# Feed-forward products by Strassen's seven products on 17 of 22 feature blocks, down products in groups of four

## The chip, the cores and the metric

The kernel runs on one core of one Trainium2 chip. TensorE does matrix products, VectorE (DVE) and ScalarE (ACT) elementwise work, POOL (GpSimd) some of it, and SyncE (SP) starts most transfers. The metric is the device time of one execution in microseconds (us).

## The reference

Two blocks of a language model in float32, for 512 tokens of width 1024. The first block has two layers. Each layer mixes tokens (a short convolution in layer 0, windowed attention in layer 1, and attention to 256 memory rows in both) and then has a feed-forward part:

```
h = rmsnorm(x, norm_ffn[i])
x = x + (silu(h @ w_gate[i]) * (h @ w_up[i])) @ w_down[i]     # 1024 -> 2816 -> 1024
```

The second block (sparse attention, retention, gated merge, output norm) follows; the change leaves its computation as it is.

## The kernel before

Activations lie transposed: `x` is eight tiles (chunks) of 128 features by 512 tokens. The 2816 features of the feed-forward part are 22 blocks of 128. Every float32 product is made of three matmuls in the chip's rounded float32 type (`mm3`, L109): each operand is split into a high part, a rounded copy by ScalarE (`copy`, L64), and a low part, the difference by VectorE (`lo_of`, L73); high x high, high x low and low x high add up in one PSUM bank. `weights` (L94) loads 128 x 1024 raw words through SP's queue into one of two raw buffers (`wr`), and writes the high and low part to one of three buffers each (`wh`, `wl`). `proj` (L115) runs the 8 x 3 matmuls of 512 columns for one 128-feature output.

`ffn` (L477) works on groups of 8, 7 and 7 blocks (`FFG`, L25). For each block it computes gate and up by `proj` from the input scaled by the norm's gain (`gained`, L202); the norm's row R (`norm_row`, L431: squares and sums on POOL, a token sum on TensorE, a reciprocal root in small steps on VectorE, a broadcast) is multiplied to each result; then comes silu on ScalarE, the product on POOL, and the split. After a group it runs the eight down products (448 or 512 words a weight row) and adds each into its chunk of `x` (L504). Between group 2 and 3 of layer 0 the keys and values of layer 1's memory attention are computed (`between`, L997, `mem_kv`, L355), with layer 1's bias tables. After the stage the next part scales all eight chunks (for layer 1's mixing twice, L508 and L511; for the second block L766) and forms the norm's row again (L509, L767).

No order is written out by hand. The library that builds the kernel fixes each engine's order when the kernel is built: what stands earlier in the program goes first, and a later instruction is put ahead where the earlier ones are not ready, as far as buffers of its tag are free. A tag's count is in `bufs` (L43, L44): `pp` 2, `lg` 3, `tp` 2 and `po` 1 PSUM banks; `t` 4 and `s` 3 work tiles. At run time each engine follows its order.

Of the kernel before, what the change touches and what calls it, by code (L numbers as in the profile page):

```python
# [24 lines left out]
FFG = [(0, 8), (8, 15), (15, 22)]  # L25


class Build:

    def __init__(self, ctx, tc, T, out):
        self.tc, self.nc, self.T, self.out = tc, tc.nc, T, out
        pool = lambda n, b, **k: ctx.enter_context(tc.tile_pool(name=n, bufs=b, **k))
        self.cst = pool("cst", 1)
        self.wp = pool("wp", 1)
        self.wbufs = dict(wr=2, wh=3, wl=3)
        self.sl = pool("sl", 1)
# [4 lines left out]
        self.bufs = dict(h=16, b=16, t=4, pa=6, pb=10, q=4, v=4, x=8, R=1, s=3, sa=1, k3=2, v3=1)  # L43
        self.pbufs = dict(pp=2, lg=3, tp=2, po=1)  # L44
# [6 lines left out]
    def slot(self, tag, dtype=F32, shape=(128, 512), name="s"):  # L51
        return self.sl.tile(list(shape), dtype, name=self.nm(name), tag=tag, bufs=self.bufs[tag])
# [287 lines left out]
    def mem_rows(self, tag="pb"):  # L340
# [12 lines left out]
        return [self.split_one(x, tag, g[:, c:c + 1], name="gm") for c, x in enumerate(chunks)]  # L353
# [123 lines left out]
    def ffn(self, layer, between=None):  # L477
        nc, T = self.nc, self.T
        h = self.gained(self.x, self.gain(2 + layer))
        R = None  # L480
        tags = ["b"] * 4 + ["pb"] * 4, ["b"] * 4 + ["pa"] * 3, ["v"] * 4 + ["q"] * 2 + ["pb"]
        for g, (f0, f1) in enumerate(FFG):
            if g == 2 and between:
                between()
            act = []
            for f in range(f0, f1):
                pg = self.psum("pp")
                self.proj(pg, T["w_gate"][layer, f], h)
                if R is None:
                    _, R = self.norm_row(1e-5, f"Rf{layer}")  # L490
                z = self.slot("t", name="z")
                self.mul(z, pg, R)
                nc.scalar.activation(z, z, AF.Silu)
                pu = self.psum("lg")
                self.proj(pu, T["w_up"][layer, f], h)
                u = self.slot("t", name="u")
                self.mul(u, pu, R)
                self.mul(u, u, z, nc.gpsimd)
                tag = tags[g][f - f0]
                act.append(self.split_one(u, tag, n=512, name="act") if tag == "v" else self.split(u, tag, name="act"))  # L500
            for c in range(8):
                ps = self.psum("po" if c % 3 == 2 else "tp")
                self.proj(ps, T["w_down"][layer, c][:, f0 * 128:f1 * 128], act)
                nc.vector.tensor_tensor(self.x[c], self.x[c], ps, op=ALU.add)  # L504
# [450 lines left out]
    def finish(self, merged):  # L955
# [3 lines left out]
        gpo = [self.slot("h", name="gpo") for _ in range(2)]  # L959
        for i in range(2):  # L960
            nc.gpsimd.dma_start(gpo[i], T["norm_post"][:, i * 512:i * 512 + 512].to_broadcast([128, 512]))
        xf = [[self.slot("h", name="xf") for _ in range(2)] for _ in range(4)]
        for tb in range(4):
            for half in range(2):
                nc.gpsimd.dma_start(xf[tb][half], self.xt[:, tb, half * 512:half * 512 + 512])
# [4 lines left out]
        for cg in range(4):  # L970
            def done(tb, ps):
                sq = self.slot("t", name="sq")[:, :256]
                nc.scalar.activation(sq, ps, AF.Square, accum_out=ss[tb][:, cg:cg + 1])
                self.mul(ys[tb][cg // 2][:, cg % 2 * 256:cg % 2 * 256 + 256], ps, gpo[cg // 2][:, cg % 2 * 256:cg % 2 * 256 + 256])

            self.proj_tok(T["w_out"][cg], merged, 256, 4, done)
        for tb in range(4):
# [6 lines left out]
            for half in range(2):  # L984
                y = ys[tb][half]
                if half and tb < 3:
                    self.copy(y, y, ri)
                    nc.gpsimd.tensor_tensor(y, y, xf[tb][half], op=ALU.add)
                else:
                    self.stt(y, y, ri, xf[tb][half], ALU.mult, ALU.add)  # L990
# [70 lines left out]
def _pack(i):  # L1061
# [64 lines left out]
```

## Time and profile before

| | before |
|---|---|
| time, median of 3 runs | 1670.27 us (1667.63 to 1670.51) |
| the profiled execution's own time | 1670.48 us |
| its span, first to last instruction | 1668.7 us |
| TensorE busy | 98% of the span, 8184 matmuls |
| VectorE, ScalarE, POOL busy | 63%, 38%, 15% |
| mean granted TensorE clock | 0.995 |

The busy time of TensorE counts an instruction from its start to its modelled end, and matmuls overlap; the distance of two starts is what one costs. `PEld` is TensorE's loading of stationary operands, beside the matmuls. L12 is a line of the kernel, often that of a helper, so that a tile's name (`wl`, `gl`, `acc`) tells more than the line.

### The profile page before, as it was taken

How to read it: one execution, taken by the hardware profiler on the slowest of the kernel's cores; microseconds unless marked ns; L12 is line 12 of the kernel's file. 1: busy time of each engine (PE TensorE's matmuls, PEld its weight loads, DVE VectorE, ACT ScalarE, POOL GpSimd, SP SyncE). 2: the span in 40 equal slices, each digit the busy share in tenths (PEclk: the TensorE clock that was granted, in tenths of full speed). 3: DMA queues.
4: the chain of work that ended last, by engine and by line, in shares of the span. 5: the costliest groups of instructions: out<-in, count | busy, mean ns of one | idle time of the engine just before them, and what ended most of it. 6: DMA issues, size and time to landing. Idle time of an engine off the chain costs nothing.

```text
span 1668.7 us, 21221 instructions
## 1 busy us (share of the span) xinstructions
PE 1634.9 (98%) x8184; PEld 1374.2 (82%) x8184; DVE 1059.2 (63%) x1828; ACT 639.0 (38%) x1134; POOL 247.1 (15%) x220
## 2 busy tenths in 40 slices
PE   8999999999999999999999999998999999999997
PEld 6888888888888788888888888878788888888887
DVE  7776745444454979875434435588788977764443
ACT  5532333222333467633222223324465533333333
POOL 1111411002011600051100101351001000010010
PEclk9999999999999999999999999999999999999999
DMA  5323222322352422122332332332401122243342
GB/s 188 118 85 102 91 98 91 101 101 85 118 160 91 159 83 84 62 102 88 101 101 95 100 109 91 101 138 93 166 28 58 45 82 83 70 151 114 126 159 88
DMA packets 51557, 171.39 MB, mean 103 GB/s; under 512 B 6680, under 2 KB 6880, under 8 KB 51328
## 3 DMA queue, kind: packets, MB, share of 16 engines
q1 hardware_dynamic: 45504, 151.11, 27.3%
q0 software_dynamic: 5376, 18.82, 3.4%
q8 instruction: 64, 1.05, 0.2%
q14 instruction: 37, 0.30, 0.1%
q10 hardware_dynamic: 576, 0.11, 0.0%
HBM read 160.56 MB, written 11.81 MB: 103 GB/s over the span
## 4 chain that ended last, share of the span: by engine, by line
PE 82%; DVE 10%; issue 2%; ACT 2%; DMA 1%; POOL 1%; DVEq 0%; SPq 0%; ACTq 0%; POOLq 0%
PE pp L112 11%; PE pp L113 11%; PE pp L111 11%; PE lg L111 8%; PE lg L112 8%; PE lg L113 7%; PE tp L112 3%; PE tp L253 2%; PE tp L113 2%; PE tp L111 2%; DVE wl L75 2%; PE po L111 2%; PE po L112 2%; PE po L113 2%; PE pp L133 2%
## 5 line engine op out<-in xcount | busy, mean ns | idle before, releaser
L65 ACT ACTIVATE wh<-wr 128x1024 fp32r<-128x1024 f32 (+2 forms) x280 | 288.5, 1030 | 695.1 <-PE pp L112 228.0
L75 DVE TENSOR_TENSOR wl<-wr,wh 128x1024 fp32r<-128x1024 f32 (+2 forms) x280 | 388.7, 1389 | 55.5 <-ACT wh L65 52.3
L111 PE MATMUL pp<-gh,wh 128*128 128x512 f32 x880 | 348.0, 396 | 7.4 <-ACT wh L65 5.9
L113 PE MATMUL pp<-gh,wl 128*128 128x512 f32 x880 | 347.2, 395 | 0.6 <-DVE wl L75 0.6
L112 PE MATMUL pp<-gl,wh 128*128 128x512 f32 x880 | 346.7, 394 | 0.5 <-DVE gl L71 0.5
L111 PEld LDWEIGHTS pp<-gh,wh 128*128 128x128 f32 x880 | 166.7, 190 | 41.4 <-ACT wh L65 6.4
L113 PEld LDWEIGHTS pp<-gh,wl 128*128 128x128 f32 x880 | 166.4, 189 | 33.9 <-DVE wl L75 1.6
L112 PEld LDWEIGHTS pp<-gl,wh 128*128 128x128 f32 x880 | 166.6, 189 | 33.2 <-DVE gl L71 1.3
L111 PE MATMUL lg<-gh,wh 128*128 128x512 f32 x408 | 159.8, 392 | 0.0
L112 PE MATMUL lg<-gl,wh 128*128 128x512 f32 x408 | 159.1, 390 | 0.0
L113 PE MATMUL lg<-gh,wl 128*128 128x512 f32 x408 | 158.8, 389 | 0.0
L68 POOL TENSOR_TENSOR u<-u,z 128x512 f32<-128x512 f32 x44 | 64.8, 1472 | 549.7 <-DVE u L68 432.6
L68 DVE TENSOR_TENSOR u<-lg,Rf 128x512 f32<-128x512 f32 x44 | 30.4, 691 | 137.4 <-PE lg L113 137.3
L112 PEld LDWEIGHTS lg<-gl,wh 128*128 128x128 f32 x408 | 76.7, 188 | 16.5 <-issue 0.7
L111 PEld LDWEIGHTS lg<-gh,wh 128*128 128x128 f32 x408 | 76.6, 188 | 16.3 <-issue 0.5
L113 PEld LDWEIGHTS lg<-gh,wl 128*128 128x128 f32 x408 | 76.6, 188 | 16.1 <-issue 0.2
L112 PE MATMUL tp<-actl,wh 128*128 128x512 f32 x216 | 84.5, 391 | 0.9 <-DVE actl L75 0.9
L111 PE MATMUL tp<-acth,wh 128*128 128x512 f32 x216 | 84.1, 389 | 0.0
L113 PE MATMUL tp<-acth,wl 128*128 128x512 f32 x216 | 84.1, 389 | 0.0
L68 DVE TENSOR_TENSOR z<-pp,Rf 128x512 f32<-128x512 f32 x44 | 30.4, 691 | 69.5 <-PE pp L113 65.7
L504 DVE TENSOR_TENSOR x<-x,tp 128x512 f32<-128x512 f32 x36 | 24.6, 683 | 65.5 <-PE tp L113 65.5
L71 DVE SCALAR_TENSOR_TENSOR gl<-x,gains,gh 128x512 fp32r<-128x512 f32 x40 | 52.9, 1338 | 0.5 <-ACT gh L65 0.5
(422 smaller groups left out, 3088.9 us busy)
## 6 DMA issues: line engine op xcount, KB each, us to landing
wr<-in_w_gate_dram SPq DMA_DIRECT2D x44, 512.0 KB, 3.2
wr<-in_w_up_dram SPq DMA_DIRECT2D x44, 512.0 KB, 3.2
wr<-in_w_in_dram SPq DMA_DIRECT2D x44, 512.0 KB, 3.2
wr<-in_w_down_dram SPq DMA_DIRECT2D x32, 448.0 KB, 3.3
wr<-in_a_w_in_dram SPq DMA_DIRECT2D x18, 512.0 KB, 3.2
wr<-in_w_down_dram SPq DMA_DIRECT2D x16, 512.0 KB, 3.5
wr<-in_a_w_out_dram SPq DMA_DIRECT2D x8, 512.0 KB, 3.2
wr<-in_b_w_q_dram SPq DMA_DIRECT2D x8, 512.0 KB, 3.2
```

The lines of the kernel that those rows point to most:

```text
L65: self.nc.scalar.activation(out, in_, AF.Copy, scale=scale)
L68: (eng or self.nc.vector).tensor_tensor(out, a, b, op=ALU.mult)
L71: (eng or self.nc.vector).scalar_tensor_tensor(out, a, s, b, op0=op0, op1=op1)
L75: self.nc.vector.tensor_tensor(out, x, hi.bitcast(F32), op=ALU.subtract)
L111: mm(ps, ah, bh, start=start, stop=False)
L112: mm(ps, ah, bl, start=False, stop=False)
L113: mm(ps, al, bh, start=False, stop=stop)
L133: mm(ps, a, wh, start=k == 0, stop=False)
L253: self.nc.tensor.transpose(ps[:, c:c + 128], src, self.ident)
L504: nc.vector.tensor_tensor(self.x[c], self.x[c], ps, op=ALU.add)
```

## The change

Five blocks (`PLAIN`) of each layer stay as they were, except that their sign is flipped and the down products are subtracted from `x`. For the other 17, gate and up together are one product of a 2 x 2 arrangement: the rows are gate and up, the inner halves are the even and odd chunks of the input, the columns are tokens 0 to 255 and 256 to 511. It is computed by seven products of 4 x 3 matmuls of 256 columns (`gate_up`), in which running sums in PSUM are copied out between products. The seven combinations of the scaled and normalised input are built once a layer after block 0 (`halves`); the weights' four sums are built for each block (`pair_weights`) and take the room of the scaled input, whose eight high and low tiles are joined to eight of 1024 columns.

The groups are 4, 4, 4, 4, 3 and 3 blocks. A group's eight down products (pairs of chunks share one weight load) run inside the blocks of the next group, after the fifth and the seventh product; those of the last group run at the end. The memory keys and values and the bias tables of layer 1 come after layer 0's stage, and use other buffers for their input. The weights are laid out anew to suit this. The last function of the kernel takes its tiles from the joined buffers (not shown).

```diff
-FFG = [(0, 8), (8, 15), (15, 22)]
+FFG = [(0, 4), (4, 8), (8, 12), (12, 16), (16, 19), (19, 22)]
+PLAIN = 5
...
     def slot(self, tag, dtype=F32, shape=(128, 512), name="s"):
+        if tag == "h":
+            shape = (128, 1024)
         return self.sl.tile(list(shape), dtype, name=self.nm(name), tag=tag, bufs=self.bufs[tag])
...
     def split(self, x, tag, scale=None, n=512, name="s"):
-        hi = self.slot(tag, F32R, name=name + "h")
-        lo = self.slot(tag, F32R, name=name + "l")
+        if tag == "h":
+            t = self.slot(tag, F32R, name=name)
+            hi, lo = t[:, :512], t[:, 512:]
+        else:
+            hi = self.slot(tag, F32R, name=name + "h")
+            lo = self.slot(tag, F32R, name=name + "l")
         self.copy(hi[:, :n], x, 1.0 if scale is None else scale)
         self.lo_of(lo[:, :n], x, hi[:, :n], scale)
...
-    def ffn(self, layer, between=None):
+    def halves(self, x, R, gain):
+        nc = self.nc
+        tags = iter(["pa"] * 6 + ["pb"] * 10 + ["q"] * 4 + ["v"] * 8)
+        spare = []
+        def slot(name):
+            tag = next(tags)
+            if tag != "v":
+                return self.slot(tag, F32R, name=name)
+            if not spare:
+                t = self.slot("v", F32R, (128, KWORDS), name)
+                spare.extend([t[:, :512], t[:, 512:1024]])
+            return spare.pop(0)
+        sub = lambda out, a, b: nc.vector.tensor_tensor(out, a, b, op=ALU.subtract)
+        sets = []
+        for j in range(len(x) // 2):
+            a, b, m, t = self.slot("t", name="b1"), self.slot("t", name="b2"), self.slot("s", name="m12"), self.slot("s", name="t34")
+            for c, o in ((2 * j, a), (2 * j + 1, b)):
+                self.stt(o, x[c], gain[:, c:c + 1], R, ALU.mult, ALU.mult)
+            b11, b12, b21, b22, m1, m2, t3, m4 = (o[:, u:u + 256] for o in (a, b, m, t) for u in (0, 256))
+            one = slot("B11")
+            self.copy(one[:, :256], b11)
+            self.lo_of(one[:, 256:], b11, one[:, :256])
+            sub(m1, b11, b12)
+            self.stt(m2, b22, -1.0, m1, ALU.mult, ALU.subtract)
+            sub(t3, b22, b12)
+            self.stt(m4, m2, -1.0, b21, ALU.mult, ALU.subtract)
+            parts = []
+            for o in (b, m, t):
+                h, l = slot("Bh"), slot("Bl")
+                self.copy(h, o)
+                self.lo_of(l, o, h)
+                parts.append(((h[:, :256], l[:, :256]), (h[:, 256:], l[:, 256:])))
+            (p21, p22), (p1, p2), (p3, p4) = parts
+            sets.append([(one[:, :256], one[:, 256:]), p21, p1, p2, p3, p22, p4])
+        return [[s[i] for s in sets] for i in range(7)]
+    def pair_weights(self, src):
+        nc = self.nc
+        k = lambda t: t.rearrange("p (k c) -> p k c", k=4)
+        raw = [self.wp.tile([128, 1120], F32, name=self.nm("wr"), tag="wr", bufs=self.wbufs["wr"])[:, :1024] for _ in range(2)]
+        for i, r in enumerate(raw):
+            nc.sync.dma_start(r, src[:, 1024 * i:1024 * i + 1024])
+        a22, a11, a12, a21 = (r[:, u:u + 512] for r in raw for u in (0, 512))
+        ah, al = (self.wp.tile([128, WMAX], F32R, name=self.nm(t), tag=t, bufs=self.wbufs[t])[:, :1024] for t in ("wh", "wl"))
+        self.copy(ah, raw[0])
+        self.lo_of(al, raw[0], ah)
+        res = {n: (k(ah[:, s]), k(al[:, s])) for n, s in (("a22", slice(0, 512)), ("a11", slice(512, 1024)))}
+        def put(name, x):
+            hi, lo = self.split(x, "h", name=name)
+            res[name] = k(hi), k(lo)
+        def put_sum(name, a, b):
+            t = self.slot("s", name=name)
+            nc.vector.tensor_tensor(t, a, b, op=ALU.add)
+            put(name, t)
+            return t
+        put("a12", a12)
+        s1 = put_sum("s1", a21, a22)
+        s2 = put_sum("s2", s1, a11)
+        put_sum("s3", a11, a21)
+        put_sum("s4", s2, a12)
+        return res
+    def gate_up(self, src, B, between):
+        nc, w = self.nc, self.pair_weights(src)
+        mm = nc.tensor.matmul
+        b11, b21, m1, m2, t3, b22, m4 = B
+        def product(ps, a, b, start):
+            for j in range(4):
+                (ah, al), (bh, bl) = (a[0][:, j], a[1][:, j]), b[j]
+                mm(ps, ah, bh, start=start and j == 0, stop=False, skip_group_check=not start)
+                mm(ps, ah, bl, start=False, stop=False, skip_group_check=not start)
+                mm(ps, al, bh, start=False, stop=j == 3, skip_group_check=not start)
+        U, Y, Z = (self.psum(t)[:, :256] for t in ("pp", "lg", "lg"))
+        g, u = self.slot("t", name="g"), self.slot("t", name="u")[:, :256]
+        g1, g2 = g[:, :256], g[:, 256:]
+        add = lambda out, a, b: nc.vector.tensor_tensor(out, a, b, op=ALU.add)
+        product(U, w["a11"], b11, True)
+        self.copy(g1, U)
+        product(Y, w["a12"], b21, True)
+        add(g1, Y, g1)
+        product(U, w["s2"], m2, False)
+        self.copy(g2, U)
+        product(Z, w["s1"], m1, True)
+        product(U, w["s3"], t3, False)
+        self.copy(u, U)
+        add(u, Z, u)
+        between(0)
+        product(Z, w["s4"], b22, False)
+        add(g2, Z, g2)
+        nc.scalar.activation(g, g, AF.Silu)
+        product(U, w["a22"], m4, False)
+        between(1)
+        act = self.slot("t", name="act")
+        self.mul(act[:, :256], U, g1)
+        self.mul(act[:, 256:], u, g2)
+        return self.split(act, "b", name="act")
...
+    def ffn(self, layer):
         nc, T = self.nc, self.T
-        h = self.gained(self.x, self.gain(2 + layer))
-        R = None
-        tags = ["b"] * 4 + ["pb"] * 4, ["b"] * 4 + ["pa"] * 3, ["v"] * 4 + ["q"] * 2 + ["pb"]
+        gain = self.gain(2 + layer)
+        h = self.gained(self.x, gain)
+        R = B = act = None
+        def down(i, act, g):
+            f0, f1 = FFG[g]
+            n = f1 - f0
+            w = []
+            def one(c):
+                if not w:
+                    w.extend(self.weights(T["w_down"][layer, i][:, f0 * 256:f1 * 256], 2 * n, 128))
+                ps = self.psum("po" if i % 2 else "tp")
+                self.proj(ps, None, act, [t[:, c * n:c * n + n] for t in w])
+                x = self.x[2 * i + c]
+                nc.vector.tensor_tensor(x, x, ps, op=ALU.subtract)
+            return [lambda: one(0), lambda: one(1)]
         for g, (f0, f1) in enumerate(FFG):
-            if g == 2 and between:
-                between()
+            last = act
+            todo = [] if last is None else [p for i in range(4) for p in down(i, last, g - 1)]
             act = []
+            share = -(-len(todo) // (f1 - max(f0, PLAIN - 1))) if todo else 0
             for f in range(f0, f1):
...
+                mine = []
+                if f >= PLAIN - 1:
+                    mine, todo = todo[:share], todo[share:]
+                def between(i):
+                    for p in mine[i * (len(mine) // 2):] if i else mine[:len(mine) // 2]:
+                        p()
+                if f < PLAIN:
+                    a, R = self.plain_gate_up(layer, f, h, R)
+                    between(0)
+                    between(1)
+                    if f == 0:
+                        B = self.halves(self.x, R, gain)
+                else:
+                    a = self.gate_up(T["w_gu"][layer, f - PLAIN], B, between)
+                act.append(a)
+        for i in range(4):
+            for p in down(i, act, len(FFG) - 1):
+                p()
...
     def run(self):
         self.load_consts()
         self.mrs = None
         self.layer_a()
-        def between():
-            loaded = self.bias_loads()
-            self.mem1 = self.mem_kv(1)
-            self.bias_tables(loaded)
-        self.ffn(0, between)
+        self.ffn(0)
+        loaded = self.bias_loads()
+        self.mem1 = self.mem_kv(1)
+        self.bias_tables(loaded)
         self.layer_b()
         self.ffn(1)
         self.second()
...
+    a["w_gate"] = np.stack([_feat(m[:, :PLAIN * 128]) for m in w["w_gate"]])
+    a["w_up"] = np.stack([_feat(m[:, :PLAIN * 128]) for m in w["w_up"]])
+    gate, up = (np.stack([_feat(m[:, PLAIN * 128:]) for m in w[n]]).reshape(2, 22 - PLAIN, 128, 4, 2, 128) for n in ("w_gate", "w_up"))
+    a["w_gu"] = np.stack([up[..., 1, :], gate[..., 0, :], gate[..., 1, :], up[..., 0, :]], 3).reshape(2, 22 - PLAIN, 128, 2048)
+    down = np.stack([_feat(m) for m in w["w_down"]]).reshape(2, 4, 2, 128, 22, 128).transpose(0, 1, 3, 2, 4, 5)
+    a["w_down"] = np.concatenate([down[:, :, :, :, f0:f1].reshape(2, 4, 128, -1) for f0, f1 in FFG], 3)
```

## Rows read from the trace of the kernel before

**Rows 1.** The page, part 1: busy us (share of the span) and instructions of each engine.

```profile
PE 1634.9 (98%) x8184; PEld 1374.2 (82%) x8184; DVE 1059.2 (63%) x1828; ACT 639.0 (38%) x1134; POOL 247.1 (15%) x220
```

**Rows 2.** TensorE's waits by line: us in total, times, longest; first and last.

```profile
PE pp L111 <- ACT wh L65: 5.9, 2, 5.7
...
PE lg L234 <- DVE q L210: 0.2, 1, 0.2
```

**Rows 3.** Windows: length, busy us of five engines, clock, DMA share, GB/s.

```profile
199.00:570.90 371.90, 371.26 (x1680) 307.63 (x1679) 193.99 (x219) 119.75 (x157) 56.39 (x48) 1.00 0.34 109
...
540.00:580.00 40.00, 39.25 (x177) 32.30 (x177) 37.94 (x37) 19.09 (x25) 29.09 (x27) 1.00 0.46 150
```

**Rows 4.** Timeline of TensorE: start us, duration us; 512-column matmuls, ten apart.

```profile
299.70 0.39 PE L111 MATMUL po<-acth,wh 128*128 128x512 f32 x1
...
301.97 0.39 PE L112 MATMUL po<-actl,wh 128*128 128x512 f32 x1
```

**Rows 5.** The same view, 256-column matmuls, eighteen apart.

```profile
451.80 0.28 PE L111 MATMUL lg<-gm,wh 128*128 128x256 f32 x1
...
453.96 0.28 PE L133 MATMUL tp<-wh,gm 128*128 128x256 f32 x1
```

**Rows 6.** Groups by line and shape: busy us, mean ns | idle before.

```profile
L65 ACT ACTIVATE wh<-wr 128x1024 fp32r<-128x1024 f32 x234 | 248.1, 1060 | 572.4 <-PE pp L112 217.7 <-PE lg L112 143.0 <-issue 84.4
...
L75 DVE TENSOR_TENSOR actl<-u,acth 128x512 fp32r<-128x512 f32 x36 | 24.5, 682 | 22.1 <-ACT acth L65 22.1
...
L65 ACT ACTIVATE acth<-u 128x512 fp32r<-128x512 f32 x36 | 22.8, 633 | 56.1 <-POOL u L68 56.1
...
L75 DVE TENSOR_TENSOR tp<-tp,tp 128x256 fp32r<-128x256 f32 x28 | 11.8, 420 | 3.1 <-ACT tp L65 2.7
...
L65 ACT ACTIVATE tp<-tp 128x256 fp32r<-128x256 f32 x28 | 10.6, 379 | 13.0 <-PE tp L253 12.9
```

**Rows 7.** Timeline of VectorE at the front of layer 0's feed-forward stage.

```profile
201.06 0.75 DVE L71 SCALAR_TENSOR_TENSOR gl<-x,gains,gh 128x512 fp32r<-128x512 f32 x1
...
206.03 0.16 DVE L68 TENSOR_TENSOR rt<-rt,m 128x4 f32<-128x4 f32 x1
206.11 1.23 DVE L75 TENSOR_TENSOR wl<-wr,wh 128x1024 fp32r<-128x1024 f32 x1
207.25 0.15 DVE L71 SCALAR_TENSOR_TENSOR rz<-rt,ri 128x4 f32<-128x4 f32 x1
```

**Rows 8.** Timeline of POOL and VectorE inside the stage.

```profile
234.81 1.29 POOL L68 TENSOR_TENSOR u<-u,z 128x512 f32<-128x512 f32 x1 [9.62 <-DVE u L68]
234.86 2.32 DVE L75 TENSOR_TENSOR wl<-wr,wh 128x1024 fp32r<-128x1024 f32 x1 [0.23 <-ACT wh L65]
```

**Rows 9.** The page, part 6: weight loads, KB each, us to landing.

```profile
wr<-in_w_gate_dram SPq DMA_DIRECT2D x44, 512.0 KB, 3.2
```

**Rows 10.** Timeline of VectorE, POOL and ScalarE around the end of layer 1.

```profile
1091.45 0.67 DVE L504 TENSOR_TENSOR x<-x,tp 128x512 f32<-128x512 f32 x1
...
1093.05 1.53 DVE L71 SCALAR_TENSOR_TENSOR gl<-x,gg,gh 128x512 fp32r<-128x512 f32 x1
...
1096.35 0.67 DVE L504 TENSOR_TENSOR x<-x,po 128x512 f32<-128x512 f32 x1
...
1109.47 0.67 DVE L157 TENSOR_TENSOR acc<-acc,sq 128x512 f32<-128x512 f32 x1
...
1092.20 1.82 POOL L148 TENSOR_TENSOR sq<-x 128x512 f32<-128x512 f32 x1 [1.24 <-DVE x L504]
...
1094.56 1.31 POOL L157 TENSOR_TENSOR acc<-acc,sq 128x512 f32<-128x512 f32 x1
...
1119.33 0.60 ACT L65 ACTIVATE R<-tp 128x512 f32<-128x512 f32 x1 [4.41 <-PE tp L197]
```

**Rows 11.** Timeline of TensorE after layer 1, and the window around it.

```profile
1110.20 1.95 PE L165 MATMUL tp<-ones,acc 128*128 128x2 f32 x16 [0.76 <-DVE acc L157]
...
1110.00:1120.00 10.00, 9.80 (x42) 7.89 (x43) 5.88 (x34) 1.66 (x2) 0.00 (x0) 0.83 0.39 133
```

More of the change, by code (lines that the diff above doesn't have):

```diff
@@ L338, in bias, with mem_rows @@
         return b
-    def mem_rows(self, tag="pb"):
+    def mem_rows(self):
         nc, T = self.nc, self.T
@@ L352, in mem_rows @@
         g = self.gain(5)
-        return [self.split_one(x, tag, g[:, c:c + 1], name="gm") for c, x in enumerate(chunks)]
+        res = []
+        for c, x in enumerate(chunks):
+            if c % 2 == 0:
+                t = self.slot("v", F32R, (128, KWORDS), "gm")
+            hi, lo = (t[:, a:a + 256] for a in (512 * (c % 2), 512 * (c % 2) + 256))
+            self.copy(hi, x, g[:, c:c + 1])
+            self.lo_of(lo, x, hi, g[:, c:c + 1])
+            res.append((hi, lo))
+        return res
     def mem_kv(self, layer):
@@ new lines, in pair_weights @@
+    def pair_weights(self, src):
[22 more added lines that the diff above has]
+        put_sum("s4", s2, a12)
+        return res
@@ new lines, in plain_gate_up @@
+    def plain_gate_up(self, layer, f, h, R):
+        T = self.T
+        pg = self.psum("pp")
+        self.proj(pg, T["w_gate"][layer, f], h)
+        if R is None:
+            _, R = self.norm_row(1e-5, f"Rf{layer}")
+        z = self.slot("t", name="z")
+        self.mul(z, pg, R)
+        self.nc.scalar.activation(z, z, AF.Silu)
+        pu = self.psum("lg")
+        self.proj(pu, T["w_up"][layer, f], h)
+        u = self.slot("t", name="u")
+        self.stt(u, pu, -1.0, R, ALU.mult, ALU.mult)
+        self.mul(u, u, z, self.nc.gpsimd)
+        return self.split(u, "b", name="act"), R
@@ L482, in ffn @@
         for g, (f0, f1) in enumerate(FFG):
-            if g == 2 and between:
-                between()
+            last = act
+            todo = [] if last is None else [p for i in range(4) for p in down(i, last, g - 1)]
             act = []
+            share = -(-len(todo) // (f1 - max(f0, PLAIN - 1))) if todo else 0
             for f in range(f0, f1):
[L487 to L504, printed above, removed]
+                mine = []
[4 more added lines that the diff above has]
+                        p()
@@ L958, in finish @@
         gf = self.gain(6)
-        gpo = [self.slot("h", name="gpo") for _ in range(2)]
+        gpo = self.slot("h", name="gpo").rearrange("p (i c) -> p i c", i=2)
         for i in range(2):
-            nc.gpsimd.dma_start(gpo[i], T["norm_post"][:, i * 512:i * 512 + 512].to_broadcast([128, 512]))
-        xf = [[self.slot("h", name="xf") for _ in range(2)] for _ in range(4)]
+            nc.gpsimd.dma_start(gpo[:, i], T["norm_post"][:, i * 512:i * 512 + 512].to_broadcast([128, 512]))
+        xf = [self.slot("h", name="xf").rearrange("p (i c) -> p i c", i=2) for _ in range(4)]
         for tb in range(4):
             for half in range(2):
-                nc.gpsimd.dma_start(xf[tb][half], self.xt[:, tb, half * 512:half * 512 + 512])
+                nc.gpsimd.dma_start(xf[tb][:, half], self.xt[:, tb, half * 512:half * 512 + 512])
         eps = self.const("eps", [128, 1])
@@ L987, in finish @@
                     self.copy(y, y, ri)
-                    nc.gpsimd.tensor_tensor(y, y, xf[tb][half], op=ALU.add)
+                    nc.gpsimd.tensor_tensor(y, y, xf[tb][:, half], op=ALU.add)
                 else:
-                    self.stt(y, y, ri, xf[tb][half], ALU.mult, ALU.add)
+                    self.stt(y, y, ri, xf[tb][:, half], ALU.mult, ALU.add)
                 nc.sync.dma_start(self.out[tb * 128:tb * 128 + 128, half * 512:half * 512 + 512], y)
```

7 lines of the change are left out of this document (2 added, 5 removed).

## The prediction

> **What bounds the kernel now.** I read the page's busy shares first, then who TensorE waits for, then the two feed-forward stages, then single matmuls. In the profiled execution (1670.48 us, span 1668.7, so 1.8 us lie around the span; the median of the runs shown is 1670.27, 0.2 us away, so a sum made on one holds for the other) TensorE is busy 98% of the span, VectorE 63%, ScalarE 38% [rows 1]. All of TensorE's waits that the trace names, 16 lines from 5.9 us down to 0.2 us, add up to 24 us [rows 2]. In layer 0's feed-forward stage it is busy 371.26 of 371.90 us while VectorE is busy 194 [rows 3]. So the stage is as long as its matmuls, and only a cheaper set of matmuls, or a new wait, moves the end. What such a matmul costs is the distance of two starts, since the printed duration overlaps with the next: ten of 512 columns take 301.97 - 299.70 = 2.27 us, 227 ns each [rows 4]; eighteen of 256 columns, each with its own weights, take 453.96 - 451.80 = 2.16 us, 120 ns each [rows 5]. Half the columns are thus 53% of the time: both are columns/2.4 GHz and 13.3 ns more.
>
> **Part 1, the products.** A feature block's gate and up take 2 x 8 x 3 = 48 matmuls of 512 columns: 48 x 0.2267 = 10.88 us. By seven products they are 7 x 4 x 3 = 84 of 256: 84 x 0.120 = 10.08 us. The gain is 0.80 us a block and, with 17 blocks in each of 2 layers, 34 x 0.80 = **27.2 us**, all on the path. The down products keep their 24 matmuls a block (5.44 us). The count of operations falls by an eighth (1.36 us of 10.88); two fifths of that go back into the 36 more matmuls.
> The rows say 13.3 ns a matmul beyond its columns [rows 4, 5]. The Trainium skill, "TensorE: Matmul & The Clock Gate" (section "Wait — 56ns, not 53.3ns?"), states about 2.5 ns for it, measured on other operands. By that figure the block would go from 10.35 to 9.17 us and the 34 blocks would give 40 us; the trace disagrees, and the measured 13.3 stands.
>
> **Part 2, what the blocks add off TensorE.** VectorE, per new block, by [rows 6, 7]: low part of 1024 weights 1.23; five low parts of 512 at 0.68; four sums of 512 at 0.68; three sums and two products of 256 at 0.42; the activation's low part 0.68; the down weights' low part 1.23; and, as the groups go from 3 to 6, two residual updates a block at 0.68 instead of one: 1.23 + 3.41 + 2.73 + 2.10 + 0.68 + 1.23 + 1.36 = 12.7 us. TensorE needs 10.08 + 5.44 = 15.5 us a block, so VectorE is 82% full and hides it. The gated product leaves POOL, which helps: beside a POOL product a low part of 1024 took 2.32 us, not 1.23 [rows 8]. ScalarE: 2 x 1.06 + 5 x 0.63 + 3 x 0.38 + 2 x 0.63 = 7.7 us, half full.
> Inside a block three matmul runs wait for a reader. The third and the fifth product write on into the bank that ScalarE copies out after the first and third; the other bank's product, 12 x 0.120 = 1.44 us, covers the copy (0.38 and two hand-overs of 0.23, as between a copy and its low part in [rows 8]: 0.84). Only where a 1.06 us weight copy stands ahead on ScalarE is it late, by up to 0.46. At none it costs 0; at both waits of each block 34 x 0.92 = 31 us. Such weight copies fill 2.1 of 15.5 us, so I take 14% x 0.23 x 2 = 0.07 a block, **+2.3 us**. The wait of the sixth product lies behind a down product of 12 x 0.227 = 2.7 us: nothing.
> The two raw weight buffers now carry three loads a block (two of the pair, one of down). The loop is: load 3.2 [rows 9], six VectorE steps until the last sum that reads the first buffer (6 x 0.68 = 4.1, and 0.8 of the running block's), down load 3.2, down's copy and low part 1.06 + 0.23 + 1.23 and a queue of 0.3: 14.1 us against 15.5. It fits with 1.4 to spare; I take 0, ends 0 and 1.0 us a block (34 us), the latter if more of the block's 5.4 us of other VectorE work falls into the loop.
>
> **Part 3, the combinations of the input.** They are built once in a layer when the norm's row R is there, and stand in the program before block 1's weights: per pair of chunks two scalings at 0.75 [rows 7], one low part, two differences and two scaled differences of 256 at 0.42, three low parts at 0.68: 5.64 us, times 4 = 22.6 us of VectorE. Then until the first new block TensorE has four plain blocks and two down products, 4 x 10.88 + 5.44 = 49 us. VectorE has in that time 22.6, 2.1 of block 0, 4 x (2 x 1.23 + 3 x 0.68) = 18, down 2.6, the first pair of weights 1.23 + 3.41 + 2.73 = 7.4 and five POOL products at 1.1 of delay [rows 8], less two low parts done ahead (2.5): 55.7 us. It is 6.7 us too much, but the pair's last sums are needed only 5.8 and 9.9 us into the block. The question is whether the plain blocks' low parts get between the combinations. Rows of the same engine say that they do: a low part of a later projection (206.11) stands between two steps of the norm (206.03, 207.25) that are earlier in the program [rows 7]. Ends: nothing; or none gets between, then TensorE has weights for block 1 alone, until 212 + 2 x 5.44 = 222.9, and waits until 212.9 + 22.6 + 1.5 = 237: 14 us a layer. I take 2 us a layer, near the lower end because of that row: **+4 us**. TensorE would start again at half clock (below).
>
> **Part 4, the ends of the layers.** The last down group is 3 blocks wide instead of 7. The eight final chunks then come every 9 x 0.227 = 2.04 us instead of 4.76, 16.3 us instead of 38. That helps nobody: the work per chunk is already VectorE's limit here. It is busy 37.9 of 40 us at the end of layer 0 [rows 3], and a chunk takes it 1091.45 to 1096.35, 4.9 us [rows 10]. Total work does not change, so it sticks out behind the last down product. End of layer 1: POOL works from 1092.20 to 1095.87, 3.7 us a chunk beside VectorE [rows 10]; I estimate 3.2 where VectorE is in its way less, so its sum is there at 2 + 8 x 3.2 = 28 us, and R 10 us after the sum (1109.47 to 1119.33): 38 us. TensorE has 16.3 of down, two projections (two banks) 10.9 and what of the value products has other banks, 6.2: 33.4. So 4.6 us of wait and 1.7 of clock: at this place TensorE waited 0.76 us, ran tiny matmuls, and was then granted 0.83 of its clock over ten us, 1.7 us lost between the levels 2.4 and 1.2 GHz [rows 11]. Before, the two were 2.5 us. Net +4. End of layer 0: VectorE needs eight updates at 0.67, four down low parts at 0.95 (between 0.68 for 512 and 1.23 for 1024), for the memory keys and values, now here, sixteen low parts of 256 at 0.42, four of 1024 weights at 1.23 and sixteen small steps at 0.16, then eight scaled low parts at 1.5 [rows 10] and two of weights at 1.23: 5.4 + 3.8 + 14.2 + 12 + 2.5 = 38 us; TensorE has 16.3 + 11.5 (96 matmuls of 256) + 5.4 = 33. Net +4. Together **+8 us**; ends -1 (the memory products fill the old 0.75 us wait and nothing sticks out) and +20 (10 each, nothing but the two projections covers).
>
> Sum: -27.2 + 2.3 + 0 + 4 + 8 = -12.9; 1670.5 - 12.9 = **1657.6 us**.
>
> **Rivals.** *All the additions hide* (VectorE's gaps suffice at the layers' fronts and ends): -27.2 + 2.3 = 1645.6. For it: VectorE idles half of the stage [rows 3]; against: it is full exactly where part 4 adds. *The ends eat more*: +20 instead of 8 gives 1669.6, no change. *The combinations hold VectorE*: 28 instead of 4 gives 1681.6, slower. It decides from the point where the stall passes 17 us in both layers together; program order speaks for it, the row at 206.11 against. *The raw-buffer loop sets the block*: from 15.5 + 0.4 us on it takes the whole net gain; at 16.5 us, 34 x 1.0 = 34: 1691.6, slower. Three loads in two buffers speak for it, the sum of 14.1 against. *The change does not cut the matmuls*, because the extra weight loads rule: the 256-column rows carry a fresh weight load each and still start every 120 ns, so I give it nothing.
>
> **Chances.** Forecast 0.41 (own range 1650 to 1665), all hidden 0.22, ends 0.10, combinations 0.14, loop 0.13. The predicted time is the forecast's, 1657.6. The range 1643 to 1687 takes in the first four and leaves out most of the loop case and the edge below. Measurement can tell about 0.2% (3.3 us) from no change: faster 0.62, same 0.11, slower 0.27.
>
> **What would show it.** Right: 9408 matmuls instead of 8184; the new products' starts 120 ns apart; VectorE about 80% full inside the stage; TensorE's busy share near 100% between about 60 us into the stage and its last block. Part 3: TensorE waits on VectorE's low parts (line of lo_of) within 40 us of R. Part 4: waits on scaled low parts or R's copy within 25 us of the last down product, with a granted clock under 1. The loop: ScalarE waiting on weight loads in every block, and TensorE on the pair's sums. The prediction is wrong if a block inside the stage takes more than 15.9 us, or if the fronts of the layers lose more than 10 us each.

## The result and the profile after

The changed kernel takes 1708.33 us (median of four executions) against 1670.28 for the kernel before beside it: ratio 1.0227, 95% interval 1.0207 to 1.0247. It is some 38 us slower; 12.9 us faster was predicted. One of the four executions was a slow one of 7116.75 us, so the ratio and every gain on the change below go by the other three (1706.03 to 1709.18, median 1707.48).

The page of the changed kernel, part 1 (answers to [rows 1]):

```profile
PE 1629.6 (95%) x9408; PEld 1423.0 (83%) x9408; DVE 1253.8 (73%) x2330; ACT 757.4 (44%) x1404; POOL 193.7 (11%) x186
```

TensorE has its 9408 matmuls and is busy 5 us less than before, in a span that is 38.6 us longer (1707.3). So it stood idle 44 us longer (77.7 against 33.8). And its busy time fell by 5 us where the products alone were to take 27.2 off: the mean granted clock is 0.979, before it was 0.995. In the two feed-forward stages it is busy 727.6 us; in e9 below, with the same number of matmuls and fewer waits, 711.8. The waits of the changed kernel, by line (answers to [rows 2], where the longest line was 5.9 us in all):

```profile
PE pp L120 <- DVE z L73: 14.0, 2, 7.0
PE pp L122 <- DVE wl L80: 8.0, 5, 7.0
PE pp L120 <- ACT wh L70: 7.6, 3, 5.6
PE pp L575 <- ACT g L70: 7.0, 4, 2.7
PE po L120 <- DVE x L638: 5.8, 5, 1.7
PE lg L122 <- DVE wl L80: 4.8, 2, 2.4
```

To place them, cut both executions at the ScalarE copy of each norm's row: Rf opens a feed-forward stage (twice), Rb layer 1's mixing, R the second block. The copies by tile (xcount: shortest/median/longest ns, first to last start in us), before and then after:

```profile
L65 ACT ACTIVATE Rf<-tp x2: 597/598/598, 210.8 to 754.6; 128x512 f32<-128x512 f32 x2
L65 ACT ACTIVATE Rb<-tp x1: 598/598/598, 583.8 to 583.8; 128x512 f32<-128x512 f32 x1
L65 ACT ACTIVATE R<-tp x1: 600/600/600, 1119.3 to 1119.3; 128x512 f32<-128x512 f32 x1
```

```profile
L70 ACT ACTIVATE Rf<-tp x2: 597/598/598, 209.9 to 777.0; 128x512 f32<-128x512 f32 x2
L70 ACT ACTIVATE Rb<-tp x1: 599/599/599, 599.2 to 599.2; 128x512 f32<-128x512 f32 x1
L70 ACT ACTIVATE R<-tp x1: 593/593/593, 1158.0 to 1158.0; 128x512 f32<-128x512 f32 x1
```

The differences give this ledger, with the kernels of the experiments below beside them (us, one profiled execution each):

| kernel | feed-forward 0 (Rf to Rb) | mixing 1 (Rb to Rf) | feed-forward 1 (Rf to R) | R to the end |
|---|---|---|---|---|
| before | 373.0 | 170.8 | 364.7 | 549.4 |
| after | 389.3 | 177.8 | 381.0 | 549.3 |
| e1 spread | 376.5 | 177.1 | 365.8 | 549.3 |
| e2 last six | 382.0 | 171.6 | 372.9 | 548.4 |
| e3 bias | 392.0 | 172.0 | 379.5 | 548.7 |
| e4 all three | 369.1 | 171.5 | 360.4 | 548.1 |
| e8 e1 and e2 | 371.8 | 171.7 | 360.5 | 549.8 |
| e11 after, squares moved | 387.2 | 171.0 | 370.7 | 552.1 |
| e9 e4, squares moved | 363.1 | 171.5 | 355.3 | 549.4 |
| e12 before, squares moved | 372.1 | 170.8 | 362.7 | 549.5 |

Each feed-forward stage is 16.3 us longer. With the 13.6 us that 17 cheaper blocks should have given, 29.9 us are lost in each, and 7.0 in layer 1's mixing, which the prediction did not look at.

**Inside the stage all is well.** TensorE's first product of two neighbouring new blocks (start, duration), and the window around them (columns as in [rows 3]):

```profile
293.30 0.28 PE L575 MATMUL pp<-B,wh 128*128 128x256 f32 x1
...
308.86 0.28 PE L575 MATMUL pp<-B,wh 128*128 128x256 f32 x1
```

```profile
290.00:550.00 260.00, 258.95 (x1773) 241.16 (x1773) 189.50 (x310) 119.89 (x199) 0.53 (x1) 1.00 0.31 101
```

A block takes 15.56 us; 15.52 was worked out. A plain block with its down products would take 72 x 0.2267 = 16.32, so a new one saves 0.76 here. VectorE is 73% busy and TensorE 258.95 of 260 us.

**The front.** VectorE of the changed kernel after layer 0's Rf (start, duration, operation; 16 us of combinations left out), TensorE beside it, and the window of both:

```profile
214.21 1.22 DVE L80 TENSOR_TENSOR wl<-wr,wh 128x1024 fp32r<-128x1024 f32 x1
217.26 0.69 DVE L80 TENSOR_TENSOR actl<-u,acth 128x512 fp32r<-128x512 f32 x1 [1.84 <-ACT acth L70]
217.87 0.42 DVE L80 TENSOR_TENSOR B<-b,B 128x256 fp32r<-128x256 f32 x1
...
234.17 0.68 DVE L73 TENSOR_TENSOR z<-pp,Rf 128x512 f32<-128x512 f32 x1
...
236.57 1.97 DVE L80 TENSOR_TENSOR wl<-wr,wh 128x1024 fp32r<-128x1024 f32 x1
```

```profile
235.00 0.77 PE L120 MATMUL pp<-g,wh 128*128 128x512 f32 x1 [6.97 <-DVE z L73]
...
238.59 0.79 PE L122 MATMUL lg<-g,wl 128*128 128x512 f32 x1 [2.40 <-DVE wl L80]
```

```profile
230.00:250.00 20.00, 12.60 (x40) 9.66 (x41) 13.42 (x20) 6.25 (x10) 3.63 (x2) 0.66 0.26 81
```

The number in brackets is the idle time before the instruction and what ended it. From 217.26 to 236 VectorE has not a gap. One low part of weights gets between the combinations (214.21), the next only at 236.57, and block 1's product with the norm's row (z) at 234.17. TensorE waits 6.97 and 2.40 us, and its mean granted clock over those 20 us is 0.66: matmuls on either side of the second wait take 0.63 us and more instead of 0.39, at 1.2 GHz.

**The end.** VectorE and GpSimd while the last down products of layer 0 run (answers to [rows 10], where a scaled low part took 1.53 us):

```profile
557.80 0.67 DVE L638 TENSOR_TENSOR x<-x,po 128x512 f32<-128x512 f32 x1
558.40 4.16 DVE L76 SCALAR_TENSOR_TENSOR g<-x,gains,g 128x512 fp32r<-128x512 f32 x2
562.49 0.74 DVE L76 SCALAR_TENSOR_TENSOR gl<-x,gains,gh 128x512 fp32r<-128x512 f32 x1
...
566.61 0.68 DVE L638 TENSOR_TENSOR x<-x,tp 128x512 f32<-128x512 f32 x1
...
570.29 2.93 DVE L76 SCALAR_TENSOR_TENSOR g<-x,gains,g 128x512 fp32r<-128x512 f32 x1
```

```profile
559.11 1.05 POOL L157 TENSOR_TENSOR sq<-x 128x512 f32<-128x512 f32 x1
...
560.69 1.31 POOL L166 TENSOR_TENSOR acc<-acc,sq 128x512 f32<-128x512 f32 x1
...
566.15 1.69 POOL L166 TENSOR_TENSOR acc<-acc,sq 128x512 f32<-128x512 f32 x1
...
570.37 1.30 POOL L166 TENSOR_TENSOR acc<-acc,sq 128x512 f32<-128x512 f32 x1
571.62 1.05 POOL L157 TENSOR_TENSOR sq<-x 128x512 f32<-128x512 f32 x1
```

The same low part takes 0.74 us at 562.49, behind the sum that ended at 562.00 and ahead of GpSimd's next square (564.56), and 2.93 at 570.29, beside a sum and a square of GpSimd (570.37 to 572.67). The update of x, which reads one of its operands from PSUM, keeps its 0.68 us at 566.61, inside a sum of GpSimd. Layer 1's end, TensorE and the ten us ahead of that wait:

```profile
1140.55 0.80 PE L122 MATMUL pp<-g,wl 128*128 128x512 f32 x1 [6.98 <-DVE wl L80]
```

```profile
1130.00:1140.00 10.00, 3.23 (x13) 2.36 (x13) 9.38 (x8) 3.01 (x4) 7.70 (x9) 0.94 0.13 52
```

**Layer 1's mixing.** Transfers of the changed kernel (KB each, middle of the us to landing), and what waited for them on ScalarE and TensorE:

```profile
band<-band POOLq DMA_DIRECT2D x1, 2304.0 KB, 13.3
...
wr<-in_w_kv_v_dram SPq DMA_DIRECT2D x2, 512.0 KB, 8.7
```

```profile
607.81 1.06 ACT L70 ACTIVATE wh<-wr 128x1024 fp32r<-128x1024 f32 x1 [7.99 <-DMA wr<-in_w_kv_v_dram]
...
608.92 0.39 PE L142 MATMUL pp<-wh,gh 128*128 128x256 f32 x1 [2.84 <-ACT wh L70]
```

The two loads went out at 593.5 and 594.9 us and the broadcast (`band`) at 594.20; the first load landed in 4.5 us, the second, behind the broadcast, in 12.8. In the kernel before the broadcast went out at 463.07, and both loads landed in 4.1.

### The profile page after: what moved, and what is told of

The parts are those of the page before. It is cut to its first block, busy times and chain, and to the rows that moved or that the text cites. A ratio compares the mean times of both kernels' runs of the same rounds, so it can differ in the third digit from the quotient of the medians.

```text
span 1707.3 us, 24407 instructions
## 1 busy us (share of the span) xinstructions
PE 1629.6 (95%) x9408; PEld 1423.0 (83%) x9408; DVE 1253.8 (73%) x2330; ACT 757.4 (44%) x1404; POOL 193.7 (11%) x186
## 3 DMA queue, kind: packets, MB, share of 16 engines
q1 hardware_dynamic: 45504, 151.11, 27.2%
## 4 chain that ended last, share of the span: by engine, by line
PE 72%; DVE 15%; DMA 5%; issue 3%; ACT 3%; POOL 1%; DVEq 0%; SPq 0%; ACTq 0%; POOLq 0%
PE pp L122 7%; PE pp L121 7%; PE pp L120 6%; PE lg L120 4%; DVE wl L80 4%; PE lg L122 4%; PE lg L121 4%; PE po L120 3%; PE pp L575 3%; PE pp L577 3%; PE pp L576 3%; PE po L121 3%; PE po L122 3%; DMA wr<-in_w_gu_dram 3%; PE tp L262 2%
## 5 line engine op out<-in xcount | busy, mean ns | idle before, releaser
L70 ACT ACTIVATE wh<-wr 128x1024 fp32r<-128x1024 f32 (+3 forms) x246 | 251.9, 1024 | 376.6 <-PE pp L121 150.5
L80 DVE TENSOR_TENSOR wl<-wr,wh 128x1024 fp32r<-128x1024 f32 (+3 forms) x246 | 315.9, 1285 | 63.3 <-ACT wh L70 62.6
L120 PE MATMUL pp<-g,wh 128*128 128x512 f32 x592 | 235.8, 399 | 21.9 <-DVE z L73 14.0
L122 PE MATMUL pp<-g,wl 128*128 128x512 f32 x592 | 235.0, 397 | 7.9 <-DVE wl L80 7.8
L121 PE MATMUL pp<-g,wh 128*128 128x512 f32 x592 | 234.4, 396 | 0.3 <-DVE g L76 0.3
L120 PEld LDWEIGHTS pp<-g,wh 128*128 128x128 f32 x592 | 112.5, 190 | 44.4 <-ACT Bh L70 14.7
L122 PEld LDWEIGHTS pp<-g,wl 128*128 128x128 f32 x592 | 112.1, 189 | 31.0 <-DVE wl L80 10.3
L121 PEld LDWEIGHTS pp<-g,wh 128*128 128x128 f32 x592 | 112.5, 190 | 21.4 <-DVE g L76 1.0
L70 ACT ACTIVATE s<-s 128x512 fp32r<-128x512 f32 x136 | 85.0, 632 | 49.2 <-DVE s L555 46.4
L80 DVE TENSOR_TENSOR s<-s,s 128x512 fp32r<-128x512 f32 x136 | 90.1, 682 | 1.0 <-ACT s L70 0.8
L575 PE MATMUL pp<-Bh,s 128*128 128x256 f32 x272 | 78.8, 290 | 7.3 <-ACT g L70 7.0
L577 PE MATMUL pp<-Bh,s 128*128 128x256 f32 x272 | 78.0, 287 | 0.0
L577 PE MATMUL lg<-Bh,s 128*128 128x256 f32 x272 | 77.0, 283 | 0.0
L575 PE MATMUL lg<-Bh,s 128*128 128x256 f32 x272 | 76.9, 283 | 0.0
L596 ACT ACTIVATE g<-g 128x512 f32<-128x512 f32 x34 | 21.4, 631 | 100.9 <-DVE g L582 100.9
```

Of the source, the lines that this page charges most:

```text
L70: self.nc.scalar.activation(out, in_, AF.Copy, scale=scale)
L80: self.nc.vector.tensor_tensor(out, x, hi.bitcast(F32), op=ALU.subtract)
L120: mm(ps, ah, bh, start=start, stop=False)
L121: mm(ps, ah, bl, start=False, stop=False)
L122: mm(ps, al, bh, start=False, stop=stop)
L575: mm(ps, ah, bh, start=start and j == 0, stop=False, skip_group_check=not start)
```

## The experiments

The theory at first: the combinations at the front, the narrow last group and the broadcast of the bias that moved behind layer 0's stage cost the some 64 us that lie between -27 and +38. Rivals: it is VectorE's total work, or the products themselves. Ratios are to the kernel before, run beside each.

**e1: combinations spread.** `halves` yields one pair of chunks at a time, and each of blocks 0 to 3 takes one:

```diff
-            sets.append([(one[:, :256], one[:, 256:]), p21, p1, p2, p3, p22, p4])
+            yield [(one[:, :256], one[:, 256:]), p21, p1, p2, p3, p22, p4]
...
-                        B = self.halves(self.x, R, gain)
+                        sets, parts = [], self.halves(self.x, R, gain)
+                    if f < 4:
+                        sets.append(next(parts))
...
```

> Only the place of the input's combinations changes: the set of one pair of chunks is built after each of the plain blocks 0 to 3, instead of all four after block 0. The work is the same. Theory A (their place in VectorE's order holds back block 1's gate row product and its weights): of the stall at each layer's front, 7.0 us for the gate product, 2.4 us for a low part and some 3 us of half clock, nearly all goes, 12 us a layer: 1708 - 24 = 1684 us. Rival B (VectorE simply has too much to do before the first new block, 55.7 us of work in 49): the wait moves to the first new block but stays, 5 to 7 us a layer less at best: 1695 to 1708 us.

1680.94 us, 1.0062 (1.0047 to 1.0077): 26.5 us less than the change, with the same operations on every engine. VectorE after the first pair:

```profile
218.53 0.69 DVE L80 TENSOR_TENSOR Bl<-b,Bh 128x512 fp32r<-128x512 f32 x1
219.13 0.68 DVE L73 TENSOR_TENSOR z<-pp,Rf 128x512 f32<-128x512 f32 x1
219.73 1.22 DVE L80 TENSOR_TENSOR wl<-wr,wh 128x1024 fp32r<-128x1024 f32 x1
```

Block 1's z comes at 219.13 instead of 234.17. The place in the program cost some 27 us, not the work. One thing e1 does not separate: z takes one of the four `t` tiles, and the combinations take two of them a pair, so as one block they stand ahead of z for tiles too. The weights' low part that follows z takes none of these tiles; its high part was begun at 217.13 in the changed kernel, and it came at 236.57 all the same.

**e2: last group of six.** The groups 3 and 3 become 6, and each of its down products takes its own weight load:

```diff
-FFG = [(0, 4), (4, 8), (8, 12), (12, 16), (16, 19), (19, 22)]
+FFG = [(0, 4), (4, 8), (8, 12), (12, 16), (16, 22)]
...
+                if n > 4:
+                    self.proj(ps, T["w_down"][layer, i][:, f0 * 256 + c * n * 128:f0 * 256 + (c + 1) * n * 128], act)
...
```

> Only the last two groups of three blocks are joined to one of six, so that the eight final chunks come every 18 x 0.227 = 4.08 us instead of 2.04; each final chunk loads its own weights. Theory A (the last chunks come faster than VectorE and POOL can take them, and TensorE waits behind): 10 us less at the end of layer 0 and of layer 1 each, R is there about 10 us earlier against the last block: 1708 - 16 = 1692 us. Rival B (the ends are long because the work after R has to be done anyway): no change beyond 3 us, 1705 to 1711.

1686.11 us, 1.0091 (1.0075 to 1.0108), 21.4 less. By the ledger 7.3 and 8.1 of it lie in the two stages and 6.2 in layer 1's mixing, where nothing was edited. There both loads go out ahead of the broadcast, at 582.0 and 583.4 against 588.69, and land in 4.3 us instead of 8.7:

```profile
band<-band POOLq DMA_DIRECT2D x1, 2304.0 KB, 11.7
...
wr<-in_w_kv_v_dram SPq DMA_DIRECT2D x2, 512.0 KB, 4.3
```

**e3: bias ahead of the first stage.**

```diff
+        self.bias_tables(self.bias_loads())
         self.ffn(0)
-        loaded = self.bias_loads()
         self.mem1 = self.mem_kv(1)
-        self.bias_tables(loaded)
```

> Only layer 1's bias tables (their loads, the product and the 2304 KB broadcast) are put before layer 0's feed-forward stage instead of behind it. Theory A (the broadcast takes the transfers' time from the value weights of the windowed attention, which landed 8.7 us after issue, and TensorE stands 7 us between Rb and Rf1): the stretch from Rb to Rf1 falls from 177.8 to 171 us: 1708 - 7 = 1701 us. Rival B (the stretch is longer because of VectorE's backlog after the stage): it stays at 177, 1707 us.

1705.32 us, 1.0205 (1.019 to 1.0221), 2.2 less: mixing 1 shrinks by 5.8, as theory A had it, and feed-forward 0 grows by 2.7 (from 389.3 to 392.0) and the time ahead of it by 1.2, which it had not.

**e4: all three, and e8: the bias put back.** e4 holds the three edits; e8 is e4 without e3's.

> The three edits together: sets spread over blocks 0 to 3, last group of six, bias tables ahead of the stage. Theory A (three separate waits): the gains add up, 24 + 16 + 7 = 47: 1661 us, below the 1670 of the kernel before, because the seven products themselves save 27 us. Rival B (VectorE's amount of work): at least 1690 us.

> As e4, with the loads and tables of the bias back behind the first FFN, where the change put them. Theory A (the broadcast of 2304 KB beside the loads of layer B's weights holds TensorE's first products there, some 3 to 6 us): e4 plus 3 to 6 us, 1666 to 1669 us. Rival B (ahead of the FFN it costs as much, in VectorE and POOL work beside the combinations, as it saves behind): within 1.5 us of e4.

e4: 1662.89 us, 0.9952 (0.9937 to 0.9967). e8: 1663.47, 0.9962 (0.9947 to 0.9976), the time that its rival B named, though not for B's reason: there is next to nothing to save behind the stage. Mixing 1 is 171.7 us in e8 with the broadcast where the change put it; it goes out at 578.90 there, behind the loads (572.1 and 573.5), which land in 4.3 us. The 7 us were a meeting of two transfers, not a price of the move. e1 and e2 together give 44.0, alone 26.5 + 21.4 = 47.9: they share some 4.

**e6: fewer of the new blocks.** e4 with `PLAIN = 13` (the block from which down products start kept at 4).

> As e4, with 13 plain feature blocks per layer instead of 5, so 9 by seven products instead of 17: 16 blocks go back, and all else (groups, halves, ends, bias) stays as in e4. Theory A (the products save what the starts say, 48 x 0.2267 = 10.88 less 84 x 0.120 = 10.08 us, 0.80 us a block, while a wait-free block stays on TensorE's pace): e4 plus 12.8 us, 1673 to 1678 us. Rival B (the seven products lose again on VectorE what they save, so that a block costs the same either way): within 3 us of e4. Rival C (they cost more than they save): below 1660 us.

1680.64 us, 1.0062 (1.0047 to 1.0077): 17.7 us more than e4 for 16 blocks, beyond the 12.8 that the starts say. TensorE's waits for x, 7.4 us in four times in e4, became

```profile
PE po L120 <- DVE x L639: 14.6, 12, 3.1
```

which is 7.2 more, while its waits for g fell from 4.7 to 0.7. Both rivals fall, and theory A's range (1673 to 1678) is passed as well. In the profiled executions e6 is 16.3 us longer than e4: 14.2 in the two stages and 2.2 behind them, where nothing was edited. Without the 3.2 us of waits that it has more, 11.0 of the 14.2 are left, near the 12.8 predicted. So e6 fits the saving, but does not measure it apart from the waits.

**e5 and e7: the waits that e4 still has.** e5 puts the last group's down products in three banks in turn; e7 adds a sixth plain block.

```diff
-                ps = self.psum("po" if i % 2 else "tp")
+                ps = self.psum("po" if (2 * i + c) % 3 == 2 and n > 4 or i % 2 and n <= 4 else "tp")
```

> As e4 (products and plain blocks as changed, halves spread over four blocks, last group of six, bias tables before the first FFN), and the down pieces of the last group go to the banks tp, tp, po in turn instead of tp, tp, po, po. Theory A (the 7.4 us that TensorE waits for x at the single po bank in e4, four times, is time on the path, with the half clock behind it): e4 less 6 to 8 us, 1655 to 1657 us, and the waits of po for x under 2 us in sum. Rival B (the subtraction of x on VectorE sets the pace of the last pieces whatever the bank, so the wait moves to tp): within 2 us of e4, 1661 to 1665 us.

> As e5, with 6 plain blocks per layer instead of 5: one more plain block between the last combination and the first block that uses them. Theory A (in e4 the first new block of a layer waits 2.3 us for ACT's copies of g, at half clock behind it, because VectorE and ACT still carry combinations): the two waits of 2.4 us go, with some 2 us of half clock each, and two blocks give back 0.8 us each, net 4 to 7 us below e5. Rival B (the wait belongs to the first of such blocks wherever it stands: its weights' seven low parts come late since nothing of it can run ahead): the wait stays at 2 us, and the kernel is 1 to 2 us slower than e5.

e5: 1662.02 us, 0.9953 (0.9938 to 0.9968), within e4's spread (1659.95 to 1664.07): theory A falls and rival B's time holds. The waits for x are gone from its list, but others stand in it:

```profile
PE tp L174 <- DVE acc L166: 4.4, 1, 4.4
PE tp L144 <- DVE wl L80: 3.7, 2, 2.9
```

e7: 1665.33, 0.9967 (0.9955 to 0.9979), 3.3 more than e5, though its runs spread (1661.43 to 1667.65). The wait for g went (5.5 to 0.8 us), but a down product of the added plain block waited instead:

```profile
279.09 0.50 PE L120 MATMUL po<-acth,wh 128*128 128x512 f32 x1 [2.10 <-DVE x L639]
```

Neither theory had it so. VectorE of e4 shows what sets the pace of the last pieces:

```profile
548.25 0.68 DVE L639 TENSOR_TENSOR x<-x,tp 128x512 f32<-128x512 f32 x1
548.84 1.21 DVE L80 TENSOR_TENSOR wl<-wr,wh 128x1024 fp32r<-128x1024 f32 x1
549.98 1.52 DVE L76 SCALAR_TENSOR_TENSOR gl<-x,gains,gh 128x512 fp32r<-128x512 f32 x1
551.43 1.90 DVE L76 SCALAR_TENSOR_TENSOR g<-x,gains,g 128x512 fp32r<-128x512 f32 x1
553.25 0.67 DVE L639 TENSOR_TENSOR x<-x,po 128x512 f32<-128x512 f32 x1
```

It has no gap, and 5.00 us from one chunk to the next, against 18 x 0.227 = 4.08 us of products. 1.9 us of the 5.00 are the two low parts' excess over 0.74. That gave a new theory: GpSimd's squares slow VectorE, and VectorE sets the end.

**e9 to e12: squares off GpSimd.** In the two norms behind a feed-forward stage ScalarE makes all squares and VectorE adds them (`act` is set in these two alone). e9 is e4 with it, e11 the changed kernel, e12 the kernel before; in e10 (e4) GpSimd keeps the sums.

```diff
-            if not first and c < last:
+            if not first and c < last and not act:
                 nc.gpsimd.tensor_tensor(sq, x, x, op=ALU.mult)
...
-                (nc.vector if first or c == last else nc.gpsimd).tensor_tensor(acc, acc, sq, op=ALU.add)
+                (nc.vector if first or act or c == last else nc.gpsimd).tensor_tensor(acc, acc, sq, op=ALU.add)
...
```

> As e4, and in the two norms that follow an FFN the squares of x and their sums are taken from GpSimd: the squares go to ScalarE, the sums to VectorE. Theory A (the last eight down pieces go at VectorE's pace, 5.03 us from one subtraction of x to the next against 4.08 us of products, because the next layer's low parts beside GpSimd's squares take 1.5 and 1.9 us where they take 0.74 alone; then the pieces go at some 4.1 us): 8 x 0.9 = 7 us less at each end, part of it hidden already, e4 less 6 to 14 us, 1649 to 1657 us, low parts at 0.75 us. Rival B (VectorE gains 0.7 us per sum to do, ScalarE gets the squares between the weight copies, and one of them holds the piece just as well): within 3 us of e4, 1660 to 1666 us.

> As e9, but the sums of the squares stay on GpSimd; only the squares go to ScalarE. Theory A: VectorE has 0.68 us less per piece than in e9, but GpSimd's sum of 1.3 us still lies beside one low part per piece and makes it about 0.7 us longer: within 3 us of e9, below e4 by 5 to 12 us. Rival B (any GpSimd work beside the pieces costs what it did): as e4, 1660 to 1666 us.

> The changed kernel itself, with e9's edit alone (squares of the two norms behind an FFN by ScalarE, sums by VectorE). Theory A (the end of an FFN is VectorE's pace against last pieces of 2.04 us of products, and about 10 us of it per end is the low parts' and weights' delay beside GpSimd, of which 5 us go into the sums that VectorE takes over): 5 us per end, 1694 to 1702 us. Rival B (the short last groups cost by their banks and loads, not by VectorE's work): within 2 us of the changed kernel, 1706 to 1710 us.

> The kernel before, with e9's edit alone. There the last pieces already go at 4.9 us from one subtraction of x to the next, against 4.76 us of products. Theory A: 8 x 0.17 us and the tail behind the last piece at each end, 1664 to 1669 us. Rival B (nothing waits there): within 1 us of the kernel before.

| run | us | ratio to before | its gain |
|---|---|---|---|
| e9 (e4 with it) | 1652.22 | 0.9892 (0.9877 to 0.9907) | 10.7 on e4 |
| e10 (sums left) | 1652.86 | 0.9897 (0.9883 to 0.9912) | 10.0 on e4 |
| e11 (after with it) | 1692.15 | 1.0131 (1.0114 to 1.0148) | 15.3 on the change |
| e12 (before with it) | 1667.28 | 0.9981 (0.9972 to 0.9991) | 2.6 on before |

The theory's times hold in e9, e10 and e12; e11 comes out below its 1694 to 1702 us, for reasons that are only in part the theory's (below). In e10 the low part that lies beside GpSimd's sum takes 1.33 to 1.63 us and the other 0.74, as it said. In e9 the same stretch of VectorE, now with the sum as well:

```profile
547.45 0.74 DVE L76 SCALAR_TENSOR_TENSOR gl<-x,gains,gh 128x512 fp32r<-128x512 f32 x1
548.12 0.68 DVE L166 TENSOR_TENSOR acc<-acc,sq 128x512 f32<-128x512 f32 x1
548.72 0.74 DVE L76 SCALAR_TENSOR_TENSOR g<-x,gains,g 128x512 fp32r<-128x512 f32 x1
549.38 0.68 DVE L639 TENSOR_TENSOR x<-x,po 128x512 f32<-128x512 f32 x1
```

More operations and less time: from gl to x it takes 1.93 us with the sum, against 3.27 without it in e4; both low parts are back at 0.74. It is the pace that gains and not the norm's tail: layer 0's last update of x comes 6.6 us earlier than in e4 (554.52 against 561.08), and Rb by as much (574.4 against 581.0).

Of e11's gain, 2.1 and 10.3 us lie in the stages and 6.8 in mixing 1; 2.8 come back at the end. Both loads go out behind the broadcast there (586.8 and 588.0 against 582.39) and land in 8.9 us, but TensorE has work until they are there. Instead it waits for a low part of weights just ahead of Rb, which the ledger counts with feed-forward 0 and which takes from that stage's gain:

```profile
586.76 0.80 PE L122 MATMUL pp<-gh,wl 128*128 128x512 f32 x1 [6.17 <-DVE wl L80]
```

e9 is the fastest version: 1.1% below the kernel before, and 15.1 below e12, the kernel before with the same cure.

## Why the prediction was wrong

- **What bounds the kernel, part 1 and part 2: right.** Block 15.56 us against 15.52 worked out, and the raw-buffer loop costs nothing: TensorE is busy 258.95 of 260 us inside the stage. e6 fits the saving by time. VectorE was 73% busy there, where about 80 was expected.
- **Part 3 failed, and with it the sign.** The step: "The question is whether the plain blocks' low parts get between the combinations. Rows of the same engine say that they do" [rows 7]. Taken: 4 us. Measured by e1: 26.5 (12.8 and 15.2 in the two stages of the profile), which is the prediction's own other end, 14 a layer; more than 10 at each front was also its sign of being wrong. The row at 206.11 was true and said something else. It stands between steps of a chain in which each waits for the one before, and such a gap takes in later work. The combinations of four independent pairs fill each other's gaps: between 217.26 and 236 VectorE has none, and nothing later in the program is put ahead until 234.17. The rival "the combinations hold VectorE" named this and was priced right (28), with a chance of 0.14.
- **Part 4 was mis-sized.** The steps: "Total work does not change" and the "3.2" us a chunk for GpSimd "where VectorE is in its way less". Taken: 8 us. Measured: 15.4 by e2 in the two stages, and on top of the wide group another 11.1 by e9 (6.0 and 5.1), of which the kernel before had 2.9 as well (e12). VectorE's time does change. The shorter products brought the chunks closer, GpSimd's squares and sums followed each other with less pause, and a low part beside them took up to 2.9 us where the part used 1.5. Most of the squares themselves were faster than before (1.05 us against 1.82 in [rows 10]), as the part had expected, while the low parts beside them took longer.
- **A cost was not named.** The move of the bias tables was in the change, and no step counted the transfers it issues: 7.0 us in layer 1's mixing. e2 and e8 lose none of it with the broadcast in the changed place, since their loads go out ahead of it; in e11 they go out behind it and TensorE has other work meanwhile. So the price depends on a few us of timing.
- **Left over.** The known costs do not add up to the whole. e1 and e2 together take 44.0 us off the change (6.1 of the transfers' 7.0 among them), and moving the squares takes 10.7 off e4, but 2.6 off the kernel before as well. Were that all, e9 would lie 27.2 us below e12; it lies 15.1 below. Of the 12 us that stay lost, 5.5 are TensorE's idle time in the two stages (6.6 us in e9 against 1.1 in e12), nearly all of it the waits for g at the first new block (2.4 and 2.6). Its busy time there falls by 21.9 us and not by 27.2; why was not tested. How much of e2's gain is the wider group and how much the loads per product was not separated either.

## What to carry to other kernels

Side work that a stage needs only later belongs into the program next to the work that may hide it, in pieces: as one block it went ahead of everything behind it, and 27 us were lost on an engine that was 73% busy. A row that shows an operation slipping between others proves it only for a chain with gaps, so look at whether the new work leaves any. Where a bound engine runs beside another one, count its operations at the duration they have beside that one; and when work moves in the program, list the transfers that move with it.

## What the runs showed of the hardware

- A VectorE low part with two operands in SBUF takes 0.74 us alone and 1.52 to 2.93 beside GpSimd's squares and sums (e4 and after), and 0.74 again when the squares and sums are off GpSimd (e9); beside the sums alone it takes 1.33 to 1.63 (e10). The update of x with one operand in PSUM keeps 0.68 beside them. Taking GpSimd out of it gave 12.4 us in the two stages of the changed kernel, and 2.6 of the one before. The Trainium skill, "SBUF — State Buffer", section "Who interferes with whom", says that a VectorE instruction with two SBUF inputs contends with a GpSimd instruction that reads SBUF; the traces agree.
- A wait of 6.97 us cost more than itself: behind it matmuls of 0.39 us took 0.63 to 0.79 until 244.3 us, and the clock granted over the 20 us around it was 0.66.
- A load of 512 KB that went out behind a broadcast of 2304 KB landed in 8.9 to 12.8 us (12.8 in the changed kernel, 12.1 in e1, 8.9 and 9.0 in e11); one that went out ahead of it took 3.6 to 4.9 (the changed kernel, e1, e2, e8).
